# A two-layer hybrid decoder on one core: the keys' RMS norm as a factor along the free axis, applied where the logits leave PSUM

## The chip, the cores and the metric

One NeuronCore of a Trainium2 chip runs the whole computation as one program. The metric is the device time of one execution in microseconds. Of the kernel before, three runs took 2642.18, 2649.83 and 2652.11 us, median 2649.83 us.

## The reference

The input is one sequence of 1024 positions by 1024 channels, float32. Layer 0 is a gated DeltaNet with a SwiGLU FFN; layer 1 is stick-breaking attention over keys and values that are computed once, again with a SwiGLU FFN. The change touches the keys of layer 1:

```python
def rms_norm(x, gain):
    y = xf * lax.rsqrt(jnp.mean(xf * xf, axis=-1, keepdims=True) + EPS)
    return (y * gain.astype(jnp.float32)).astype(x.dtype)
...
    k, v = jnp.split(rms_norm(h, kv_norm) @ w_kv, 2, axis=-1)
    k = rms_norm(k.reshape(b_, s_, SB_HEADS, SB_DH), k_gain).transpose(0, 2, 1, 3)
...
        z = jnp.einsum('bhtd,bhsd->bhts', qb, kb) * scale
        ls_neg = jax.nn.log_sigmoid(-z)
        log_fail = jnp.where(causal, ls_neg, 0.0)
        log_rest = lax.cumsum(log_fail, axis=3, reverse=True) - log_fail
        log_a = z + ls_neg + log_rest
        att = jnp.where(causal, jnp.exp(log_a), 0.0)
```

There are 8 heads of 128 channels. A key's norm is one number for each head and each position s, so in the logits z[t, s] it is a factor that depends on the column s alone.

## The kernel before

The program runs in four stages: the DeltaNet mixer, its FFN, the attention ("sba") and the second FFN. Products that must be exact are made as three products of float32r parts, high by high, high by low and low by high, so a projection of one head (128 output channels, one half of 512 positions) is 8 times three products of 512 columns into a PSUM tile `ups` (`proj_half`, L135). Each engine executes its instructions in the order in which the program issues them.

In the attention stage (from L1458) the generators of one head's attention, `sb_steps(hd)`, and of the next head's projections, `qkv_steps(hd + 1)`, are interleaved by `merge` according to the costs that they yield. Work that hangs on a projection is put off by `post(delay, fn)` and taken up by `with_posts` once the projections' own clock has passed it.

- `k_take` (L1524) before the change: the head's keys, positions along the free axis and channels along the partitions, are copied to SBUF (L1550). `norm` transposes four blocks of 128 by 128 on PE (L1488), `row_norm` squares them on ACT (L1493), sums the rows on DVE (L1494) and takes (mean + EPS) to the power -0.5 on POOL with operands of 128x4 (L1495, L1496). `scale` multiplies the transposed keys by it on DVE (L1538). `back` transposes them back (L1488) and splits them with the gain into `kh` (L1545, ACT) and `kl` (L1546, DVE). That is done for each half of each head, 16 times.
- `sb_logs` (L1578): for block tb of 128 queries, the logits of up to 512 keys at a time in a PSUM tile `ips` (L1590 to L1592), out of which ACT takes the absolute value with the query's norm as scale into `l` (L1593) and DVE the scaled logits into `z` (L1594); then Exp and Ln over `l` (L1598, L1599).
- `sb_weights` (L1602): DVE adds max(z, 0) to `l` (L1607), POOL sets the part of the diagonal block that is not causal with two `affine_select` instructions of 128x128, first in `l`, then in `z` (L1609), DVE scans `l` backwards (L1613) and subtracts it from `z` (L1614), ACT takes Exp of `z` (L1616).
- `sb_transpose` (L1619) transposes `z` on PE (L1629) for the product with the values (`sb_values`, L1635). Block k's logits stand beside the weights of block k - 1, the transposes of block k - 2 and the values of block k - 3 (`sb_order`).
- `col_unit` (L115): a projection's raw weights are multiplied by the gain on POOL in four instructions of 128x256 (L121) before they are split.

POOL's power with a -0.5 operand is used in other places too: with 128x1 operands in the norms of rows (L208), with 128x4 in the DeltaNet mixer (L1176, L1321). PSUM has three tiles `ups` and five tiles `ips`.

Of the kernel before, what the change touches and what calls it, by code (L numbers as in the profile page):

```python
# [9 lines left out]
F32 = mybir.dt.float32  # L10
F32R = mybir.dt.float32r
U8 = mybir.dt.uint8
AF = mybir.ActivationFunctionType
ALU = mybir.AluOpType
# [4 lines left out]
P = 128  # L19
EPS = 1e-6  # L20
# [3 lines left out]
def yoco_kernel(  # L24
# [22 lines left out]
    act, dve, pool, pe, sp = nc.scalar, nc.vector, nc.gpsimd, nc.tensor, nc.sync  # L47
# [10 lines left out]
    HB = S // 2  # L58
# [16 lines left out]
    def i_tile(shape=(P, 4, P)):  # L75
        return pi.tile(list(shape), F32, tag="i", name="ips")

    def n_tile(shape=(P, S)):
        return main.tile(list(shape), F32, tag="n", name="n", bufs=4)
# [4 lines left out]
    def bc(ap, n=P):  # L84
        return ap.unsqueeze(2).broadcast_to([ap.shape[0], ap.shape[1], n])
# [4 lines left out]
    ones = cpool.tile([P, 1], F32, name="ones")  # L90
    pool.memset(ones, 1.0)
    mhalf = cpool.tile([P, 4], F32, name="mhalf")
# [78 lines left out]
    def run(gen):  # L171
        for _ in gen:
            pass
# [803 lines left out]
    with tc.tile_pool(name="gdn", bufs=1) as gp:  # L977
# [50 lines left out]
        def gain_cols(i, j, n):  # L1028
            return gains[:, offs[i] + j * n : offs[i] + (j + 1) * n]
# [4 lines left out]
        g_k = gain_cols(4, 0, 1)  # L1034

        norm = Norm(g_attn[0], False)
# [407 lines left out]
    with tc.tile_pool(name="ffn0", bufs=1) as hp:  # L1444
        norm, norm1 = PairNorm(g_ffn[0], hp), Norm(None)
# [12 lines left out]
    with tc.tile_pool(name="sba", bufs=1) as ap_:  # L1458
        tc.keep_in_program_order(act.preload_act_table_set("natural_log_exp_and_others"))

        def sb_tile(tag, nm):
            return ap_.tile([P, S], F32R, tag=tag, name=nm, bufs=4 if tag != "v" else 3)

        posts, clock = [], [0]
        POST, SCALE, BACK = 3000, 2000, 3000

        def post(delay, fn, *args):
            posts.append((clock[0] + delay, fn, args))
            posts.sort(key=lambda p: p[0])
# [15 lines left out]
        def transpose_half(f, hf):  # L1485
            tps = i_tile()
            for j in range(4):
                pe.transpose(tps[:, j, :], f[:, hf * HB + j * P : hf * HB + (j + 1) * P], ident)  # L1488
            return tps

        def row_norm(s_, tps):
            sq = main.tile([P, 4, P], F32, tag="og", name="sq")
            act.activation(sq, tps, AF.Square, scale=float(P) ** -0.5)  # L1493
            dve.tensor_reduce(s_, sq, axis=AX.X, op=ALU.add)  # L1494
            pool.tensor_scalar(s_, s_, EPS, None, op0=ALU.add)  # L1495
            pool.tensor_tensor(s_, s_, mhalf, op=ALU.pow)  # L1496

        def z_tile(tag):
            return ap_.tile([P, S], F32, tag=tag, name=tag, bufs=3 if tag == "z" else 2)

        def f_tile(hd):
            return z_tile("z") if hd == 0 else n_tile()

        def q_take(hd):
# [16 lines left out]
            qkv[hd, "q"] = (hi, lo, ss)  # L1521
            return take

        def k_take(hd):  # L1524
            f = f_tile(hd)
            hi, lo = sb_tile("k", "kh"), sb_tile("k", "kl")
            qkv[hd, "k"] = (hi, lo)

            def norm(hf):
                tps = transpose_half(f, hf)  # L1530
                ss = ap_.tile([P, 4], F32, tag="ss", name="ss", bufs=4)
                row_norm(ss, tps)
                post(SCALE, scale, hf, tps, ss)
                return 436

            def scale(hf, tps, ss):
                fs = f[:, hf * HB : (hf + 1) * HB].rearrange("p (a b) -> p a b", b=P)
                dve.tensor_tensor(fs, tps, bc(ss), op=ALU.mult)  # L1538
                post(BACK, back, hf)
                return 1  # L1540

            def back(hf):
                hs = slice(hf * HB, (hf + 1) * HB)
                tf = transpose_half(f, hf).rearrange("p a b -> p (a b)")
                act.activation(hi[:, hs], tf, AF.Copy, scale=g_k)  # L1545
                dve.scalar_tensor_tensor(lo[:, hs], tf, g_k, hi[:, hs], op0=ALU.mult, op1=ALU.subtract)  # L1546
                return 436

            def take(hf, sl, ps):
                act.copy(f[:, sl], ps)  # L1550
                post(POST, norm, hf)

            return take

# [18 lines left out]
        qkv, zs, ats, ofs = {}, {}, {}, {}  # L1573
# [3 lines left out]

        def sb_logs(hd, tb, later):  # L1578

            (qh, ql, qs), (kh, kl) = qkv[hd, "q"], qkv[hd, "k"]  # L1580
            w = (tb + 1) * P
            ts_ = slice(tb * P, (tb + 1) * P)
            z, l = z_tile("z"), z_tile("l")
            sc = qs[:, tb : tb + 1]
            next(later, None)
            for s0 in range(0, w, 512):
                n = min(512, w - s0)
                ss_ = slice(s0, s0 + n)
                zps = i_tile((P, 512))
                pe.matmul(zps[:, :n], qh[:, ts_], kh[:, ss_], start=True, stop=False)  # L1590
                pe.matmul(zps[:, :n], qh[:, ts_], kl[:, ss_], start=False, stop=False)
                pe.matmul(zps[:, :n], ql[:, ts_], kh[:, ss_], start=False, stop=True)  # L1592
                act.activation(l[:, ss_], zps[:, :n], AF.Abs, scale=sc)  # L1593
                dve.tensor_scalar(z[:, ss_], zps[:, :n], sc, None, op0=ALU.mult)  # L1594
                yield 3 * max(107, n * 0.417)
                next(later, None)
            run(later)
            act.activation(l[:, :w], l[:, :w], AF.Exp, scale=-1.0)  # L1598
            act.activation(l[:, :w], l[:, :w], AF.Ln, bias=1.0)  # L1599
            chains[hd, tb] = (z, l)  # L1600
# [53 lines left out]
        def sb_order():  # L1654

            blocks = [(hd, tb) for hd in range(H) for tb in range(NT)]
            n = len(blocks)
            for k in range(n + 3):
                at_ = blocks[min(k, n - 1)][0]
                later = sb_weights(*blocks[k - 1]) if 1 <= k < n + 1 else iter(())  # L1660
                yield at_, sb_logs(*blocks[k], later) if k < n else later
                if 2 <= k < n + 2:
                    yield at_, sb_transpose(*blocks[k - 2])
                if k >= 3 and blocks[k - 3][1] % 2:
                    hd, tb = blocks[k - 3]
                    yield at_, sb_values(hd, tb // 2)
# [14 lines left out]
        def head_all(hd):  # L1681
            takes = [k_take, q_take, v_take]
            if hd == 0:
                yield from proj_two_steps(norm1, [(la1.ready.pop(0), takes.pop(0)(hd)) for _ in range(2)])
                la1.fill(2)
            for take in takes:
                last = hd == H - 1 and take is takes[-1]
                for i, cost in enumerate(proj_steps(xT, la1.get(), take(hd))):
                    yield cost
                    if last and i in (1, KT + 1):  # L1690
                        next(fill)
# [39 lines left out]
    with tc.tile_pool(name="ffn1", bufs=1) as hp:  # L1731
        norm = PairNorm(g_ffn[1], hp)
# [34 lines left out]
```

## Time and profile before

| What | Value |
|---|---|
| runs of the kernel before, median | 2649.83 us |
| profiled execution, its own time | 2648.18 us |
| profiled execution, span | 2646.5 us |
| PE busy | 2539.9 us, 96% |
| DVE busy | 1844.0 us, 70% |
| ACT busy | 1144.9 us, 43% |
| POOL busy | 859.4 us, 32% |
| attention stage | about 1405 us to 1890 us |

The profile is of one execution, with times in microseconds from the span's start. PE is the engine of the matrix products, DVE the vector engine, ACT the scalar engine, POOL the general one, PEld the loading of weights into PE. Matmuls are pipelined, so the distance between two starts tells the cost of a product and not its listed duration. The profiled execution took 1.65 us less than the median.

### The profile page before, as it was taken

What the parts mean: (1) busy time and instruction counts of PE and PEld (TensorE: products, weight loads), DVE (VectorE), ACT (ScalarE), POOL (GpSimd) and SP (SyncE); (2) the same over time, 40 slices, a digit from 0 to 9 for tenths busy, and PEclk for the clock granted to TensorE, in tenths of its full rate; (3) what the DMA queues carried; (4) which work ended last, traced back from release to release, by engine and by line L of the source; (5) the groups of instructions that cost most, each with busy time, mean ns of one, the idle gap of its engine ahead of it and who ended that gap; (6) DMA issues with size and microseconds to landing.
All of it is one profiled execution on the core that took longest, in us unless ns stands there. A gap on an engine that the chain in (4) does not pass through costs nothing. (4 is left out here: it accounts for less than half of the span.)

```text
span 2646.5 us, 35828 instructions
## 1 busy us (share of the span) xinstructions
PE 2539.9 (96%) x12908; PEld 2067.5 (78%) x12908; DVE 1844.0 (70%) x2721; ACT 1144.9 (43%) x2219; POOL 859.4 (32%) x1262
## 2 busy tenths in 40 slices
PE   8999999999999999998999999999899999999999
PEld 6777878787768888886777778887776888887777
DVE  6667766775686666677755788877768566666774
ACT  6333333334363444432215666666536444443220
POOL 2444444444411222154313343342320222215420
PEclk9999999999999999999999999999999999999999
DMA  4211212223324554578661111112232455448766
GB/s 122 65 58 54 66 54 65 66 72 102 132 64 144 170 145 135 162 253 291 235 214 64 40 33 33 40 33 72 99 133 84 119 164 164 142 138 285 276 224 203
DMA packets 368952, 331.77 MB, mean 125 GB/s; under 512 B 19571, under 2 KB 321790, under 8 KB 368774
## 3 DMA queue, kind: packets, MB, share of 16 engines
q1 hardware_dynamic: 368774, 329.48, 39.5%
q8 instruction: 101, 1.65, 0.3%
q14 instruction: 77, 0.63, 0.1%
HBM read 226.37 MB, written 103.06 MB: 124 GB/s over the span
## 5 line engine op out<-in xcount | busy, mean ns | idle before, releaser
L140 PE MATMUL ups<-x,wh 128*128 128x512 f32 (+1 forms) x912 | 389.4, 428 | 0.0
L142 PE MATMUL ups<-x,wl 128*128 128x512 f32 (+1 forms) x912 | 363.6, 399 | 0.0
L141 PE MATMUL ups<-x,wh 128*128 128x512 f32 (+1 forms) x912 | 359.9, 395 | 0.0
L453 PE MATMUL ips<-x,w 128*128 128x512 f32 x840 | 328.7, 393 | 7.4 <-ACT x L359 3.7
L454 PE MATMUL ips<-x,w 128*128 128x512 f32 x840 | 329.1, 392 | 2.3 <-DVE x L360 2.3
L455 PE MATMUL ips<-x,w 128*128 128x512 f32 x840 | 328.3, 391 | 0.0
L552 POOL TENSOR_TENSOR n<-n,ev 128x512 f32<-128x512 f32 x44 | 70.7, 1606 | 626.5 <-ACT n L551 626.5
L453 PE MATMUL ups<-x,w 128*128 128x512 f32 x648 | 252.0, 392 | 1.7 <-ACT x L359 1.7
L454 PE MATMUL ups<-x,w 128*128 128x512 f32 x648 | 253.1, 391 | 0.0
L455 PE MATMUL ups<-x,w 128*128 128x512 f32 x648 | 252.3, 389 | 0.0
L142 PEld LDWEIGHTS ups<-x,wl 128*128 128x128 f32 (+1 forms) x912 | 171.1, 188 | 37.7
L453 PEld LDWEIGHTS ips<-x,w 128*128 128x128 f32 x840 | 157.8, 188 | 46.6 <-ACT x L359 6.2
L140 PEld LDWEIGHTS ups<-x,wh 128*128 128x128 f32 (+1 forms) x912 | 172.0, 189 | 22.7
L141 PEld LDWEIGHTS ups<-x,wh 128*128 128x128 f32 (+1 forms) x912 | 172.4, 189 | 21.3 <-DVE x L232 0.2
L454 PEld LDWEIGHTS ips<-x,w 128*128 128x128 f32 x840 | 158.3, 188 | 38.3 <-DVE x L360 4.9
L455 PEld LDWEIGHTS ips<-x,w 128*128 128x128 f32 x840 | 158.2, 188 | 32.9
L746 DVE TENSOR_TENSOR h<-h,ips 128x512 f32<-128x512 f32 x176 | 119.3, 682 | 61.0 <-PE ips L455 60.8
L453 PEld LDWEIGHTS ups<-x,w 128*128 128x128 f32 x648 | 121.5, 188 | 29.2 <-ACT x L359 4.0
L454 PEld LDWEIGHTS ups<-x,w 128*128 128x128 f32 x648 | 121.8, 188 | 26.8 <-DVE x L360 1.6
L455 PEld LDWEIGHTS ups<-x,w 128*128 128x128 f32 x648 | 121.7, 188 | 25.0
L746 DVE TENSOR_TENSOR h<-h,ups 128x512 f32<-128x512 f32 x136 | 92.6, 682 | 46.5 <-PE ups L455 46.3
L104 DVE TENSOR_TENSOR wl<-raw,wh 128x1024 fp32r<-128x1024 f32 x64 | 82.9, 1295 | 57.4 <-ACT wh L103 56.7
(364 smaller groups left out, 5991.7 us busy)
## 6 DMA issues: line engine op xcount, KB each, us to landing
raw<-in_ffn_w_gu_dram SPq DMA_DIRECT2D x88, 512.0 KB, 4.5
w<-hsa SPq DMA_DIRECT2D x88, 512.0 KB, 4.7
hsa<-w SPq DMA_DIRECT2D x116, 256.0 KB, 2.9
hb<-hsb SPq DMA_DIRECT2D x68, 384.0 KB, 4.0
raw<-in_ffn_w_down_dram SPq DMA_DIRECT2D x44, 512.0 KB, 4.3
raw<-in_gdn_w_in_dram SPq DMA_DIRECT2D x32, 512.0 KB, 4.1
hsb<-w SPq DMA_DIRECT2D x54, 256.0 KB, 3.6
hsa<-n SPq DMA_DIRECT2D x48, 256.0 KB, 3.6
```

What stands on the lines that cost most here:

```text
L104: dve.tensor_tensor(lo, raw, hi, op=ALU.subtract)
L140: pe.matmul(o, wh[:, kt, :m], xh, start=kt == 0, stop=False)
L141: pe.matmul(o, wh[:, kt, :m], xl, start=False, stop=False)
L142: pe.matmul(o, wl[:, kt, :m], xh, start=False, stop=kt == KT - 1)
L453: pe.matmul(ps, ah, bh, start=start, stop=False, skip_group_check=True)
L454: pe.matmul(ps, ah, bl, start=False, stop=False, skip_group_check=True)
L455: pe.matmul(ps, al, bh, start=False, stop=stop, skip_group_check=True)
L552: pool.tensor_tensor(s, s, self.t3, op=ALU.mult)
L746: dve.tensor_tensor(d, d, ps, op=ALU.add)
```

## The change

The keys are no longer normed before the logits. `kh` and `kl` are split straight from the projection's PSUM tile with the gain alone. Beside that ACT writes the squares, divided by 128, into a tile `sq`. `norm` sums them over the partitions by one float32 product with ones of 128x128 and 512 columns, so that every partition holds the sum of each position; ACT adds EPS on the way out of PSUM, and POOL takes the result to the power -0.5 in place, as a tile of 128x512 with the exponent broadcast. The tile `rk` so made (one tile for each head; a tile of tag `n`, for all heads but the first the same tile as `sq`) is a factor of the logits as they leave PSUM: one DVE instruction multiplies by the query's norm and by `rk`, and ACT takes the absolute value from `z` in SBUF afterwards.

```diff
-        POST, SCALE, BACK = 3000, 2000, 3000
+        POST = 3000
...
+        eps = ap_.tile([P, 1], F32, name="eps")
+        pool.memset(eps, EPS)
+
         def k_take(hd):
-            f = f_tile(hd)
+
             hi, lo = sb_tile("k", "kh"), sb_tile("k", "kl")
-            qkv[hd, "k"] = (hi, lo)
+            sq = f_tile(hd)
+            rk = [None if hd == 0 else sq]
+            qkv[hd, "k"] = (hi, lo, rk)
 
             def norm(hf):
-                tps = transpose_half(f, hf)
-                ss = ap_.tile([P, 4], F32, tag="ss", name="ss", bufs=4)
-                row_norm(ss, tps)
-                post(SCALE, scale, hf, tps, ss)
-                return 436
-
-            def scale(hf, tps, ss):
-                fs = f[:, hf * HB : (hf + 1) * HB].rearrange("p (a b) -> p a b", b=P)
-                dve.tensor_tensor(fs, tps, bc(ss), op=ALU.mult)
-                post(BACK, back, hf)
-                return 1
-
-            def back(hf):
                 hs = slice(hf * HB, (hf + 1) * HB)
-                tf = transpose_half(f, hf).rearrange("p a b -> p (a b)")
-                act.activation(hi[:, hs], tf, AF.Copy, scale=g_k)
-                dve.scalar_tensor_tensor(lo[:, hs], tf, g_k, hi[:, hs], op0=ALU.mult, op1=ALU.subtract)
-                return 436
+                if rk[0] is None:
+                    rk[0] = n_tile()
+                ms = i_tile((P, HB))
+                pe.matmul(ms, ones.broadcast_to([P, P]), sq[:, hs], start=True, stop=True)
+                act.activation(rk[0][:, hs], ms, AF.Identity, bias=eps)
+                pool.tensor_tensor(rk[0][:, hs], rk[0][:, hs], mhalf[:, 0:1].broadcast_to([P, HB]), op=ALU.pow)
+                return 908
 
             def take(hf, sl, ps):
-                act.copy(f[:, sl], ps)
-                post(POST, norm, hf)
+                act.activation(sq[:, sl], ps, AF.Square, scale=float(P) ** -0.5)
+                act.activation(hi[:, sl], ps, AF.Copy, scale=g_k)
+                dve.scalar_tensor_tensor(lo[:, sl], ps, g_k, hi[:, sl], op0=ALU.mult, op1=ALU.subtract)
+                post(POST if hd else 2 * POST, norm, hf)
 
             return take
...
-            (qh, ql, qs), (kh, kl) = qkv[hd, "q"], qkv[hd, "k"]
+            (qh, ql, qs), (kh, kl, (rk,)) = qkv[hd, "q"], qkv[hd, "k"]
...
-                act.activation(l[:, ss_], zps[:, :n], AF.Abs, scale=sc)
-                dve.tensor_scalar(z[:, ss_], zps[:, :n], sc, None, op0=ALU.mult)
+                dve.scalar_tensor_tensor(z[:, ss_], zps[:, :n], sc, rk[:, ss_], op0=ALU.mult, op1=ALU.mult)
+                act.activation(l[:, ss_], z[:, ss_], AF.Abs)
```

The other costs that `norm` returns move the steps of `merge` against each other. The rows below are of the attention of head 2 and the projections of head 3, a pair of streams that stands for those of the heads after it. A tile's number tells one buffer's use from another; the numbers differ between the kernels.

POOL, before the change, from the third block of head 2 (`l_14487`, `z_14486`) to the sixth (`l_14684`); `ss` is the norm of the keys of head 3, `raw` a raw weight:

```order
L1609 AFFINE_SELECT l_14487<-l_14487 128x128
L1609 AFFINE_SELECT z_14486<-z_14486 128x128
L1495 TENSOR_SCALAR ss_14534<-ss_14534 128x4
L1496 TENSOR_TENSOR ss_14534<-ss_14534,mhalf_76 128x4
L1609 AFFINE_SELECT l_14571<-l_14571 128x128
L1609 AFFINE_SELECT z_14570<-z_14570 128x128
L121 TENSOR_TENSOR raw_15174<-raw_15174,gains_123 128x256 x4
L1609 AFFINE_SELECT l_14616<-l_14616 128x128
L1609 AFFINE_SELECT z_14615<-z_14615 128x128
L1495 TENSOR_SCALAR ss_14658<-ss_14658 128x4
L1496 TENSOR_TENSOR ss_14658<-ss_14658,mhalf_76 128x4
L1609 AFFINE_SELECT l_14684<-l_14684 128x128
```

POOL, after the change, the same place: `l_14414` is the third block of head 2, `l_14487` now the fourth, `l_14534` the fifth, and `n_14301` is the tile `rk` of head 3:

```order
L1606 AFFINE_SELECT l_14414<-l_14414 128x128
L1606 AFFINE_SELECT z_14413<-z_14413 128x128
L1541 TENSOR_TENSOR n_14301<-n_14301,mhalf_76 128x512
L1606 AFFINE_SELECT l_14487<-l_14487 128x128
L1606 AFFINE_SELECT z_14486<-z_14486 128x128
L121 TENSOR_TENSOR raw_15069<-raw_15069,gains_123 128x256 x4
L1541 TENSOR_TENSOR n_14301<-n_14301,mhalf_76 128x512
L1606 AFFINE_SELECT l_14534<-l_14534 128x128
L1606 AFFINE_SELECT z_14533<-z_14533 128x128
```

The power of four columns has become one of 512, in front of the selects of the fourth and of the fifth block; between the two powers stand the selects of one block and the four instructions of one raw weight.

DVE, after the change, from the fourth block's `l` to the place behind the fifth block's subtraction (L1610 is the scan, L1611 the subtraction, L1590 the eviction of logits, `attl` the low part of transposed weights):

```order
L1604 SCALAR_TENSOR_TENSOR l_14487<-z_14486,l_14487 128x512
L1590 SCALAR_TENSOR_TENSOR z_14533<-ips_14554,ssq_13953,n_13737 128x128
L1610 SCALAR_TENSOR_TENSOR l_14487<-l_14487 128x512
L1629 TENSOR_TENSOR attl_14564<-ips_14565,atth_14563 128x3x128
L1611 TENSOR_TENSOR z_14486<-z_14486,l_14487 128x512
L1604 SCALAR_TENSOR_TENSOR l_14534<-z_14533,l_14534 128x640
L1590 SCALAR_TENSOR_TENSOR z_14587<-ips_14594,ssq_13953,n_13737 128x512
L1610 SCALAR_TENSOR_TENSOR l_14534<-l_14534 128x640
L1611 TENSOR_TENSOR z_14533<-z_14533,l_14534 128x640
L1590 SCALAR_TENSOR_TENSOR z_14587<-ips_14608,ssq_13953,n_13737 128x256
```

Each scan reads what POOL's select has written, and the evictions of PSUM tiles behind it on DVE follow it in order, as they did before. On PE, from the first product with ones of head 3 to the transposes of the fourth block (`z_14486`) stand 39 products of 512 columns, 18 of 256, 9 of 128, five transposes and the second product with ones; to the transposes of the fifth block (`z_14533`) four transposes, 15 products of 512 and 3 of 384 columns more.

PE, after the change, the end of the stretch to the fourth block's transposes:

```order
L1643 MATMUL ips_14575<-atth_14434,vh_14200 128x256
L1644 MATMUL ips_14575<-attl_14435,vh_14200 128x256
L1645 MATMUL ips_14575<-atth_14434,vl_14201 128x256
L1539 MATMUL ips_14579<-n_14301,ones_74 128x512
...
L1587 MATMUL ips_14608<-kh_13735,qh_13951 128x256
L1588 MATMUL ips_14608<-kl_13736,qh_13951 128x256
L1589 MATMUL ips_14608<-kh_13735,ql_13952 128x256
L1626 MATMUL ips_14617<-ident_69,z_14486 128x128 x4
```

The second product with ones stands ahead of the transposes that need the selects behind the first power.

## Rows read from the trace of the kernel before

**Rows 1.** The page, busy time of two engines (share of span, instructions):

```profile
PE 2539.9 (96%) x12908; PEld 2067.5 (78%) x12908; DVE 1844.0 (70%) x2721; ACT 1144.9 (43%) x2219; POOL 859.4 (32%) x1262
```

**Rows 2.** Stretches: us, busy us (instructions) by engine, PE clock; one head, an early stretch.

```profile
core 0: us, PE busy (x) PEld busy (x) DVE busy (x) ACT busy (x) POOL busy (x), PEclk, DMA share, GB/s
1502.45:1560.12 57.67, 54.93 (x309) 46.67 (x309) 45.79 (x63) 38.71 (x71) 20.28 (x33) 1.00 0.12 37
...
50.00:60.00 10.00, 8.39 (x43) 6.81 (x42) 8.51 (x13) 5.12 (x16) 0.10 (x1) 0.83 0.38 109
```

**Rows 3.** Waits, 1405 to 1890 us: who waited for whom: us, times, longest.

```profile
POOL l L1609 <- DVE l L1607: 176.1, 44, 9.4
...
DVE l L1613 <- POOL l L1609: 21.9, 29, 2.4
...
PE ips L1590 <- DVE kl L1546: 6.3, 6, 1.2
...
PE ips L1488 <- DVE n L1538: 1.6, 1, 1.6
```

**Rows 4.** Single lines, POOL's powers and a multiply: ns minimum, median, maximum; starts.

```profile
L208 POOL TENSOR_TENSOR nss<-nss,mhalf x32: 549/569/1018, 5.6 to 1986.7; 128x1 f32<-128x1 f32 x32
...
L1496 POOL TENSOR_TENSOR ss<-ss,mhalf x16: 1037/1038/1044, 1410.4 to 1812.5; 128x4 f32<-128x4 f32 x16
...
L1177 POOL TENSOR_SCALAR rk<-rk x16: 223/230/252, 62.5 to 608.5; 128x4 f32<-128x4 f32 x16
```

**Rows 5.** Groups by form, POOL: out<-in, shape, count | busy us, mean ns | idle before.

```profile
L552 POOL TENSOR_TENSOR n<-n,ev 128x512 f32<-128x512 f32 x44 | 70.7, 1606 | 626.5 <-ACT n L551 626.5
...
L1217 POOL TENSOR_TENSOR um<-tc,mdiag 128x512 f32<-128x512 f32 x16 | 20.7, 1295 | 1.3
...
L1215 POOL TENSOR_TENSOR tc<-tc,pr 128x60 f32<-128x60 f32 x16 | 5.0, 315 | 1.3
...
L1215 POOL TENSOR_TENSOR tc<-tc,pr 128x4 f32<-128x4 f32 x16 | 3.4, 212 | 1.2
```

**Rows 6.** Groups by form, POOL: raw weights by the gain, and the select.

```profile
L121 POOL TENSOR_TENSOR raw<-raw,gains 128x256 f32<-128x256 f32 x96 | 77.2, 833 | 74.5 <-DMA raw<-in_w_kv_dram 58.9 <-DMA raw<-in_sb_w_q_dram 8.6 <-ACT n L1650 4.0
...
L1609 POOL TENSOR_SCALAR_AFFINE_SELECT l<-l 128x128 f32<-128x128 f32 x64 | 19.1, 299 | 176.1 <-DVE l L1607 176.1
```

**Rows 7.** Groups by form, 1270 to 1960 us: DVE's scan and subtraction, ACT.

```profile
L1613 DVE TENSOR_TENSOR_SCAN l<-l 128x640 f32<-128x640 f32 x8 | 12.3, 1536 | 6.6 <-POOL l L1609 6.6
...
L1614 DVE TENSOR_TENSOR z<-z,l 128x640 f32<-128x640 f32 x8 | 6.5, 812 | 0.0
...
L1493 ACT ACTIVATE sq<-ips 128x512 f32<-128x512 f32 x32 | 19.2, 600 | 14.0 <-PE ips L1488 14.0
...
L1616 ACT ACTIVATE z<-z 128x640 f32<-128x640 f32 x8 | 5.9, 740 | 14.7 <-DVE z L1614 14.7
```

**Rows 8.** Timeline of PE in head 1's attention: start us, duration us, line, out<-in.

```profile
1504.48 0.60 PE L1629 MATMUL ips<-ident,z 128*128 128x128 f32 x4
1504.83 0.48 PE L140 MATMUL ups<-x,wh 128*128 128x512 f32 x1
1505.15 0.39 PE L141 MATMUL ups<-x,wh 128*128 128x512 f32 x1
1505.38 0.39 PE L142 MATMUL ups<-x,wl 128*128 128x512 f32 x1
1505.61 0.34 PE L1590 MATMUL ips<-kh,qh 128*128 128x384 f32 x1
1505.79 0.35 PE L1591 MATMUL ips<-kl,qh 128*128 128x384 f32 x1
...
1508.01 0.28 PE L1646 MATMUL ips<-atth,vh 128*128 128x256 f32 x1
1508.13 0.28 PE L1647 MATMUL ips<-attl,vh 128*128 128x256 f32 x1
```

**Rows 9.** Timeline of PE in the first stage: four float32 products of 128 columns.

```profile
328.36 1.05 PE L1143 MATMUL ips<-y 128*128 128x128 f32 x8
329.17 0.47 PE L140 MATMUL ups<-x,wh 128*128 128x512 f32 x1
```

## The prediction

> **What bounds the kernel now.** I read the page's busy times first: PE is busy in 96% of the span, POOL in 32% [rows 1]. By stretches, one head of the attention takes 57.67 us, in which PE is busy 54.93, DVE 45.79, ACT 38.71 and POOL 20.28 us [rows 2]. So PE sets the pace, and a gain has to come out of PE's work or PE's waits. The view of waits tells what little waiting there is. PE lost 6.3 us to `kl` and 1.6 us to the scaled keys in the whole stage; DVE's scan waited 21.9 us for POOL's select; and POOL waited 176.1 us for the input of that select [rows 3]. The reader is to see in this that POOL has much idle time, but that it stands inside the chain of every block: DVE's `l`, POOL's selects, DVE's scan and subtraction, ACT's Exp, PE's transposes. Idle time of such an engine is room for many short instructions and for no long one, since it works in order.
>
> **The change part by part.** The largest question is the new power on POOL, 128x512, 16 times. The nearest rows are powers of the same kind on narrower tiles: 569 ns for one column and 1038 ns for four, with minimum and median a few ns apart for the wide one [rows 4]. Three columns more cost 469 ns, 156.3 ns each. That is not what POOL takes for other things: a multiply or add of four columns takes 212 to 230 ns [rows 4, 5], one of 60 columns 315 and one of 512 columns 1295 [rows 5], (1295 - 212) / 508 = 2.1 ns a column. So the power has a price by the column, some 73 times that of a multiply, and nothing in the narrow rows says that it ends at four. Drawn on: 569 + 511 x 156.3 ns = 80.5 us for each. The bounds lie far apart. Below, a power costs a multiply's 1.6 us [rows 5]; above, four columns are the unit of work and all of it repeats, 1038 / 4 = 259.5 ns a column, 133 us. I take 80.5, because it is the line through the two rows of the same operation.
>
> [...]
>
> What of a power lies on the path: the selects behind it wait, the scan waits for them on DVE with evictions behind it, and PE comes to the transposes of that block and stops. I follow one pair of powers, from the end of the first product with ones, for the heads 2 to 7. ACT takes the sums out of PSUM in 0.6 us (as the squares [rows 7]); the power 80.5; two selects 0.6 and the raw weight's four instructions 3.3 [rows 6]; the second power, whose input has long been ready, 80.5; then a select 0.3 [rows 6], the scan of 640 columns 1.54, the subtraction 0.81, Exp 0.74 [rows 7], together 3.4. That is 168.9 us, after which PE may transpose the fifth block. PE has other work up to there: 54 products of 512 columns at 0.23 us from start to start, 3 of 384 at 0.18, 18 of 256 at 0.12, four transposes in 0.35 us, so 9 of them in 0.8 [rows 8], 9 of 128 columns, which I put at 0.1 between 256 columns and nothing, and the second product with ones, 0.81 by four float32 products of 128 columns [rows 9]: 12.4 + 0.5 + 2.2 + 0.8 + 0.9 + 0.8 = 17.6 us. The pair adds 168.9 - 17.6 = 151.3 us; six of them 907.8. The evictions that PE needs within these 17.6 us stand ahead of the waiting scans on DVE, or the five PSUM tiles suffice for them.
>
> The pair of head 1 has more on PE up to the first transposes behind its second power (137 products of 512 columns, 3 of 384, 27 of 256, 9 of 128, 34 transposes, one product with ones: 40.1 us by the same prices). The pair of head 0 runs before any attention and its first transposes come after 113 of 512, 3 each of 384, 256 and 128, 16 transposes and one product with ones: 29.4 us. Their POOL rows differ by some microseconds (wider blocks, a weight more), so I use 168.9 for both: 128.8 and 139.5. All eight: 907.8 + 128.8 + 139.5 = **1176 us**.
>
> The smaller terms. On PE a half of the keys loses eight transposes, twice 0.35 us [rows 8], and gains the product with ones, 0.81 [rows 9]: 0.1 us more, 16 times, 1.6 us. The waits for the scaled keys and for `kl` [rows 3] can go: 7.9 us less at most, which I take. [...] Eight returns after the second powers: 0 to 14 us, and I take 14. [...] DVE loses a reduction and a multiply for each half, ACT exchanges a copy for the evicted sums: both stay below PE's 54.93 us a head [rows 2], so I cost them at nothing; without PE's cover DVE would be next, at 45.79. The absolute value now follows the logits' eviction and does not run beside it, which lengthens a block's chain by less than the 0.6 us of an ACT pass [rows 7], two blocks ahead of its transposes: nothing. `rk` keeps a tile of tag `n` for a whole head; if a later tile had to wait for it, that would be a loss, which I leave to the upper end. No DMA is added or moved; raw weights behind a power come late, but their split is due after the stop that the power causes anyway.
>
> Sum: 1176 + 1.6 - 7.9 + 14 = 1184 us. The profiled execution took 2648.2 us, 1.65 below the median of the runs: 2648.2 + 1184 = **3832 us**. A tenth more or less in the price of a column moves this by 16 x 8 = 128 us, and if PE's work covers nothing, it rises by 6 x 17.6 + 40.1 + 29.4 = 175 us. So this case reaches by itself from 3700 to 4007 us.
>
> **The rivals.** First, a power of 512 columns is as cheap as a multiply, 1.6 us. Then POOL keeps its idle time, the selects wait 1.6 us at most where they waited before for a power of 1.04, and the product with ones and the ended waits remain: 2648.2 + 1.6 - 7.9 = 2642 us, not slower. It decides from the point at which a power is short against the 13 us of PE work ahead of the first transposes (39 products of 512 columns, 18 of 256, 9 of 128, five transposes, one with ones). For it speaks that all other two-input work of POOL is cheap and that much of 569 ns may be a start; against it, the difference of 469 ns for three columns, in which no start is left.
>
> Second, long rows are cheaper by the column than short ones, say by half (an unrolled loop that four columns don't fill): 0.6 + 511 x 0.078 = 40.5 us, 40 us less for each of 16, and 3832 - 640 = 3192 us. With other fractions anything from 2700 to 3700. For it speaks only that four columns are few; against it, that multiplies keep the same price from 4 and 60 to 512 columns.
>
> Third, the cover is gone: DVE stands at the scan, the PSUM tiles behind it fill, and PE stops at once. That is the 175 us above: 4007 us. Against it speaks that four PSUM tiles of five are taken when PE gets to the transposes.
>
> **How the numbers follow.** My forecast has 0.75, the cheap power 0.08, the half price 0.12, the lost cover 0.05. About 0.5% of the time, 13 us, is what a measurement of this kernel can tell from no change. The cheap power's 2642 us lies within that; with some waits more gone it may pass below 2635, so of its 0.08 I put 0.06 on the same and 0.02 on faster. All else is slower: 0.92. The range goes from 3300 to 4010: nearly all of the forecast's case (0.73), a third of the half price (0.04), more than half of the lost cover (0.03), 0.80 together. The forecast's own range is 3700 to 4007.
>
> **What would show it.** The new power as a group of 16 on POOL with a mean near 80 us; POOL busy near 2100 us; PE busy still near 2540 us, but two thirds of the span; in the waits DVE's scan for POOL's select as the largest, near 1100 us, with ACT's Exp and PE's transposes behind it; eight pairs of stops in the attention stage, each near 150 us, at a lowered PE clock after them. Wrong would be: a mean of a few us, a mean that is not near 156 ns times 512, or PE idle time much below or above what the powers last.

## The result, and the profile after

The changed kernel takes 3880.03 us (median of five runs, 3877.75 to 3880.81) against 2649.83 us, the median of five as well: 1.4652 times the time before, 95% interval 1.4633 to 1.4671. The forecast was 3832 us in a range from 3300 to 4010. The profiled execution took 3877.85 us, 1229.7 more than that of the kernel before.

The page's busy times and its costliest groups answer to [rows 1] and [rows 4]; in the groups the columns are line, engine, operation, shapes and count, then busy us and mean ns of one, then the idle time before them and what ended it:

```profile
PE 2573.1 (66%) x12812; PEld 2084.4 (54%) x12812; DVE 1835.9 (47%) x2689; ACT 1139.2 (29%) x2219; POOL 2153.4 (56%) x1247
...
L1541 POOL TENSOR_TENSOR n<-n,mhalf 128x512 f32<-128x512 f32 x16 | 1317.2, 82328 | 13.6 <-ACT n L1540 13.6
L1626 PE MATMUL ips<-ident,z 128*128 128x128 f32 x288 | 55.3, 311 | 1069.7 <-ACT z L1613 1069.7
L1610 DVE TENSOR_TENSOR_SCAN l<-l 128x128 f32<-128x128 f32 (+3 forms) x64 | 89.2, 1394 | 1198.1 <-POOL l L1606 1197.8
```

Sixteen powers take 82.3 us each, 1317 us in all, and POOL's busy time grew by 1294 us from 859.4: the powers are the whole of it. PE has about the work it had and is now busy in 66% of the span. The idle time moved to the chain behind POOL: DVE's scan waits 1197.8 us for POOL's select, where it waited 21.9 before [rows 3], and PE's transposes wait 1069.7 us for ACT's Exp, which comes after the scan.

One pair of powers in POOL's timeline (start us, duration us, line, out<-in, and in brackets the idle time before), of the attention of head 3 with the powers of head 4:

```profile
2236.16 0.29 POOL L1606 TENSOR_SCALAR_AFFINE_SELECT z<-z 128x128 f32<-128x128 f32 x1
2236.42 82.57 POOL L1541 TENSOR_TENSOR n<-n,mhalf 128x512 f32<-128x512 f32 x1
2318.96 0.29 POOL L1606 TENSOR_SCALAR_AFFINE_SELECT l<-l 128x128 f32<-128x128 f32 x1
2319.20 0.29 POOL L1606 TENSOR_SCALAR_AFFINE_SELECT z<-z 128x128 f32<-128x128 f32 x1
2319.46 4.35 POOL L121 TENSOR_TENSOR raw<-raw,gains 128x256 f32<-128x256 f32 x4
2323.77 81.91 POOL L1541 TENSOR_TENSOR n<-n,mhalf 128x512 f32<-128x512 f32 x1
2405.65 0.29 POOL L1606 TENSOR_SCALAR_AFFINE_SELECT l<-l 128x128 f32<-128x128 f32 x1
...
2450.64 82.57 POOL L1541 TENSOR_TENSOR n<-n,mhalf 128x512 f32<-128x512 f32 x1
```

PE's timeline in the same pair:

```profile
2234.14 1.02 PE L1539 MATMUL ips<-n,ones 128*128 128x512 f32 x2
2234.59 0.68 PE L1643 MATMUL ips<-atth,vh 128*128 128x256 f32 x1
2235.11 0.28 PE L1644 MATMUL ips<-attl,vh 128*128 128x256 f32 x1
...
2248.36 0.28 PE L1589 MATMUL ips<-kh,ql 128*128 128x256 f32 x1
2322.33 1.12 PE L1626 MATMUL ips<-ident,z 128*128 128x128 f32 x4 [73.69 <-ACT z L1613]
2323.10 0.78 PE L140 MATMUL ups<-x,wh 128*128 128x512 f32 x1
...
2328.10 0.40 PE L142 MATMUL ups<-x,wl 128*128 128x512 f32 x1
2409.28 1.11 PE L1626 MATMUL ips<-ident,z 128*128 128x128 f32 x4 [80.78 <-ACT z L1613]
```

The reader is to see two stops, 73.69 and 80.78 us, each in front of the transposes of a block whose select stood behind a power. Between the product with ones and the first stop PE has its 13.6 us of other work, between the two stops 6. From one head's first power (2236.42) to the next (2450.64) pass 214.2 us; before, a head took 57.67 [rows 2].

The stretches of that head (us; busy us and instructions of each engine; PE's granted clock; DMA share; GB/s):

```profile
2235.00:2321.00 86.00, 13.64 (x74) 11.26 (x72) 10.22 (x15) 8.87 (x17) 85.08 (x7) 0.59 0.04 12
2321.00:2329.00 8.00, 6.16 (x22) 4.92 (x22) 2.43 (x4) 2.00 (x4) 8.00 (x4) 0.71 0.00 0
2329.00:2409.00 80.00, 0.00 (x0) 0.00 (x0) 2.92 (x4) 0.51 (x1) 77.19 (x3) 0.52 0.00 0
2409.00:2420.00 11.00, 10.72 (x50) 9.22 (x50) 9.00 (x13) 8.93 (x17) 2.95 (x6) 0.75 0.00 1
2420.00:2449.30 29.30, 28.46 (x155) 23.49 (x154) 20.03 (x27) 17.72 (x35) 10.79 (x17) 1.00 0.13 37
```

While PE stands in the third stretch, its granted clock is 0.52 of full; behind the second stop it is 0.75 over eleven microseconds, 0.50 from 2409.28 to 2414.40 among them, and then 1.00. In the third stretch POOL alone is at work, 77.19 of 80 us; DVE has 2.92, ACT 0.51 and PE nothing.

The powers of head 1, beside head 0's attention, stop PE at other places. Of the waits in the stage (who waited for whom: us, times, longest), two single ones are theirs, and DVE's timeline shows what held the first:

```profile
PE ips L1488 <- ACT n L1565: 80.2, 10, 73.7
...
PE ips L1539 <- DVE attl L1629: 75.4, 1, 75.4
...
1685.06 1.82 DVE L1610 TENSOR_TENSOR_SCAN l<-l 128x768 f32<-128x768 f32 x1 [78.45 <-POOL l L1606]
1686.81 0.66 DVE L1629 TENSOR_TENSOR attl<-ips,atth 128x512 fp32r<-128x512 f32 x1
```

Here PE stops already at the second product with ones (L1539), because DVE stands at the scan and the copy `attl`, which frees a PSUM tile, stands behind that scan. So the second power's input is late, and the two powers of this head lie 7.4 us apart, where those of head 4 lie 4.8. The second stop, 73.7 us, is at the transposes of the values, which wait for ACT's copy behind Exp.

### The profile page after: what moved, and what is told of

It reads as the page before. It is cut to its first block, busy times and chain, and to the rows that moved or that the text cites. A ratio compares the mean times of both kernels' runs of the same rounds, so it can differ in the third digit from the quotient of the medians.

```text
span 3876.1 us, 35606 instructions
## 1 busy us (share of the span) xinstructions
PE 2573.1 (66%) x12812; PEld 2084.4 (54%) x12812; DVE 1835.9 (47%) x2689; ACT 1139.2 (29%) x2219; POOL 2153.4 (56%) x1247
## 5 line engine op out<-in xcount | busy, mean ns | idle before, releaser
L1541 POOL TENSOR_TENSOR n<-n,mhalf 128x512 f32<-128x512 f32 x16 | 1317.2, 82328 | 13.6 <-ACT n L1540 13.6
L1626 PE MATMUL ips<-ident,z 128*128 128x128 f32 x288 | 55.3, 311 | 1069.7 <-ACT z L1613 1069.7
L1610 DVE TENSOR_TENSOR_SCAN l<-l 128x128 f32<-128x128 f32 (+3 forms) x64 | 89.2, 1394 | 1198.1 <-POOL l L1606 1197.8
L1626 PEld LDWEIGHTS ips<-ident,z 128*128 128x128 f32 x288 | 39.6, 158 | 1084.7 <-ACT z L1613 1077.6
L1613 ACT ACTIVATE z<-z 128x128 f32<-128x128 f32 (+3 forms) x64 | 43.7, 683 | 1253.2 <-DVE z L1611 1253.2
L140 PE MATMUL ups<-x,wh 128*128 128x512 f32 (+1 forms) x912 | 397.0, 436 | 0.0
L141 PE MATMUL ups<-x,wh 128*128 128x512 f32 (+1 forms) x912 | 366.0, 402 | 0.0
L140 PEld LDWEIGHTS ups<-x,wh 128*128 128x128 f32 (+1 forms) x912 | 176.7, 194 | 25.1 <-issue 0.5
L141 PEld LDWEIGHTS ups<-x,wh 128*128 128x128 f32 (+1 forms) x912 | 176.7, 194 | 23.9 <-issue 0.5
```

The source lines that it names most:

```text
L140: pe.matmul(o, wh[:, kt, :m], xh, start=kt == 0, stop=False)
L141: pe.matmul(o, wh[:, kt, :m], xl, start=False, stop=False)
L1541: pool.tensor_tensor(rk[0][:, hs], rk[0][:, hs], mhalf[:, 0:1].broadcast_to([P, HB]), op=ALU.pow)
L1610: dve.tensor_tensor_scan(rv, rv, rv, 0.0, op0=ALU.add, op1=ALU.bypass)
L1613: act.activation(z[:, :w], z[:, :w], AF.Exp)
L1626: pe.transpose(tps[:, j, :], z[:, (j0 + j) * P : (j0 + j + 1) * P], ident)
```

## The experiments

The theory was that POOL's power has a price by the column, and that everything behind it on an engine that works in order waits for it. The rivals: that a part of the loss lies in the rest of the change; that the price is one of the instruction or of the stop and not of the columns.

### The power as a multiply

```diff
-                pool.tensor_tensor(rk[0][:, hs], rk[0][:, hs], mhalf[:, 0:1].broadcast_to([P, HB]), op=ALU.pow)
+                pool.tensor_tensor(rk[0][:, hs], rk[0][:, hs], mhalf[:, 0:1].broadcast_to([P, HB]), op=ALU.mult)
```

> The changed kernel with one word changed: POOL multiplies the 512 columns by the broadcast operand where it took them to a power, so the keys' norm is left out and all else of the change stays. Theory of the prediction (the price of a power by the column, in front of selects on an engine that works in order, is the whole loss): the new instruction takes 1.3 to 1.6 us and the time falls from 3880 to 2642 us, between 2630 and 2655. Rival (a good part of the 1230 us comes from the rest of the change: the product with ones, the eviction on DVE with the absolute value behind it, the tile kept for a head): above 2680 us, with PE waits in the attention stage that the kernel before did not have.

Measured: 2657.76 us against 2648.78, ratio 1.0034 (1.0022 to 1.0047). One word, with which the kernel leaves out the keys' norm, takes 1222 of the 1230 us away. The group of 16 on POOL is now

```profile
L1541 POOL TENSOR_TENSOR n<-n,mhalf 128x512 f32<-128x512 f32 x16 | 22.7, 1418 | 15.6 <-ACT n L1540 15.6
```

1.4 us in place of 82.3. But the time lies 3 us over the range that was expected: what is left of the change, POOL's multiply of 512 columns included, is not the gain of 6 us that was reckoned but costs 9 us.

### The power on half of the columns

```diff
-                pool.tensor_tensor(rk[0][:, hs], rk[0][:, hs], mhalf[:, 0:1].broadcast_to([P, HB]), op=ALU.pow)
+                h0 = slice(hf * HB, hf * HB + HB // 2)
+                pool.tensor_tensor(rk[0][:, h0], rk[0][:, h0], mhalf[:, 0:1].broadcast_to([P, HB // 2]), op=ALU.pow)
```

> The changed kernel with the power on the first 256 of each half's 512 columns only; the other 256 keep mean plus EPS, so half of the keys are not normed. Price by the column at 160 ns: 41.3 us for each of 16, 41 us less each, 16 x 41 = 656 us less: 3224 us. Rival one (the instruction has a large fixed part): over 3500 us. Rival two (fewer columns are hidden better, since PE's own work covers a fixed 17 us of a pair): that cover is already full, so no difference from the first.

Measured: 3229.29 us in one run, where 3224 was expected. Half of the columns took about half of the loss away. The group:

```profile
L1542 POOL TENSOR_TENSOR n<-n,mhalf 128x256 f32<-128x256 f32 x16 | 664.5, 41532 | 13.7 <-ACT n L1540 13.7
```

Each power is 82.3 - 41.5 = 40.8 us shorter; 16 of them make 653 us, and the time fell by 651. A microsecond of power was a microsecond of the kernel, so the cover by PE's own work is indeed used up already and the same for both.

### The price at eight widths

```diff
+        probe = half("um").rearrange("p a b -> p (a b)")
+        pool.memset(probe, 3.7)
+        pool.tensor_tensor(probe[:, 0:1], probe[:, 0:1], mhalf[:, 0:1].broadcast_to([P, 1]), op=ALU.pow)
...
+        pool.tensor_tensor(probe[:, 0:256], probe[:, 0:256], mhalf[:, 0:1].broadcast_to([P, 256]), op=ALU.mult)
```

> The kernel before, with powers of 1, 2, 4, 8, 16, 64, 256 and 512 columns of a tile of 3.7 and multiplies of 4, 16 and 256 columns added on POOL at the start, none of them used. A straight line through 569 ns for one and 1038 ns for four columns gives 0.57, 0.73, 1.04, 1.66, 2.9, 10.4, 40.4 and 80.5 us. Rival (short rows pay a start that long ones don't, or long rows cost more by the column): the wide ones lie off the line; 41.6 us at 256 and 82.3 at 512, read already from two kernels, would put the step between 4 and 256 columns. Multiplies: 0.2, 0.3 and 0.8 us.

The groups by shape, POOL, of that kernel (the last two are multiplies):

```profile
L993 POOL TENSOR_TENSOR um<-um,mhalf 128x1 f32<-128x1 f32 x1 | 0.6, 552 | 0.0
...
L994 POOL TENSOR_TENSOR um<-um,mhalf 128x2 f32<-128x2 f32 x1 | 0.9, 853 | 0.0
...
L995 POOL TENSOR_TENSOR um<-um,mhalf 128x4 f32<-128x4 f32 x1 | 1.0, 1018 | 0.1
...
L996 POOL TENSOR_TENSOR um<-um,mhalf 128x8 f32<-128x8 f32 x1 | 1.6, 1634 | 0.1
...
L997 POOL TENSOR_TENSOR um<-um,mhalf 128x16 f32<-128x16 f32 x1 | 2.9, 2894 | 0.1
...
L998 POOL TENSOR_TENSOR um<-um,mhalf 128x64 f32<-128x64 f32 x1 | 10.5, 10518 | 0.1
...
L999 POOL TENSOR_TENSOR um<-um,mhalf 128x256 f32<-128x256 f32 x1 | 41.1, 41125 | 0.1
...
L1000 POOL TENSOR_TENSOR um<-um,mhalf 128x512 f32<-128x512 f32 x1 | 81.9, 81915 | 0.1
...
L1001 POOL TENSOR_TENSOR um<-um,mhalf 128x4 f32<-128x4 f32 x1 | 0.2, 201 | 0.1
...
L1003 POOL TENSOR_TENSOR um<-um,mhalf 128x256 f32<-128x256 f32 x1 | 1.0, 995 | 0.1
```

It is a straight line but for the row of two columns, which lies 0.15 us over it: (1018 - 552) / 3 = 155 ns a column at the narrow end, (81915 - 41125) / 256 = 159 at the wide end. No width is clearly cheaper by the column than the line says. A multiply of 256 columns takes 1.0 us, a power 41.1. The whole kernel took 2787.89 us in one run, 140 us over the runs beside it. That is the sum of these powers, which stand between the first norms' short powers on POOL.

### Four pieces for each power, spread over the blocks

```diff
-                pool.tensor_tensor(rk[0][:, hs], rk[0][:, hs], mhalf[:, 0:1].broadcast_to([P, HB]), op=ALU.pow)
+                for j in range(4):
+                    post(2500 * j + 5000 * hf, piece, hf * HB + j * P)
                 return 908

+            def piece(c):
+                cs = slice(c, c + P)
+                with ExitStack() as es:
+                    if sel[0] is not None:
+                        es.enter_context(tc.issue_after(sel[0].ins))
+                    pool.tensor_tensor(rk[0][:, cs], rk[0][:, cs], mhalf[:, 0:1].broadcast_to([P, P]), op=ALU.pow)
+                return 1
```

> The changed kernel with each power of 512 columns made as four of 128 that are spread over the blocks of the head before: on POOL there stand two, one, two and three of them between the selects of successive blocks. The same columns are taken to the power, so POOL works as long. Theory (a stop costs what POOL takes less the PE work that runs under it): four stops a head in place of two have some 7 us of PE work each under them, so a head falls from 214 by some 15 us, and the time by some 100 to 130: 3750 to 3790 us. Rival (what counts is that PE stops at all, with a price for each stop in clock and drained queues): not faster than 3880, and up to 3950 us.

Measured: 3799.9 us, ratio 1.4345 (1.4318 to 1.4373), 80 us less than the changed kernel. POOL's timeline of one head:

```profile
2012.61 42.06 POOL L1551 TENSOR_TENSOR n<-n,mhalf 128x128 f32<-128x128 f32 x2
...
2059.95 21.88 POOL L1551 TENSOR_TENSOR n<-n,mhalf 128x128 f32<-128x128 f32 x1
...
2082.30 42.83 POOL L1551 TENSOR_TENSOR n<-n,mhalf 128x128 f32<-128x128 f32 x2
...
2127.04 63.81 POOL L1551 TENSOR_TENSOR n<-n,mhalf 128x128 f32<-128x128 f32 x3
...
2213.72 21.36 POOL L1551 TENSOR_TENSOR n<-n,mhalf 128x128 f32<-128x128 f32 x1
```

A head takes 2213.72 - 2012.61 = 201.1 us in place of 214.2, 13 less (15 expected). PE has four stops a head here in place of two. More stops with PE work under each are better than fewer, so the rival of a price for each stop falls. The whole gain is 80 us and not 100 to 130: six heads at 13 us make it, and the first two give nothing (their stops last 147 and 152 us, before 145 and 149). The expectation also took POOL to work as long as before, but 64 pieces of 21.2 us hold it for 1358 us, 41 more than the sixteen powers.

### Ln and Exp on ACT

```diff
-                act.activation(rk[0][:, hs], ms, AF.Identity, bias=eps)
-                pool.tensor_tensor(rk[0][:, hs], rk[0][:, hs], mhalf[:, 0:1].broadcast_to([P, HB]), op=ALU.pow)
+                act.activation(rk[0][:, hs], ms, AF.Ln, bias=eps)
+                act.activation(rk[0][:, hs], rk[0][:, hs], AF.Exp, scale=-0.5)
```

> The changed kernel with the power taken off POOL: ACT takes Ln of the sums plus EPS on the way out of PSUM and then Exp with scale -0.5, so the norm is computed in full by another engine. If POOL's power is the whole loss: one ACT pass of 0.6 us more for each of 16 halves, on an engine that is busy 38.7 of 57.7 us a head, so nothing on the path: 2642 us, between 2630 and 2655, as the multiply. Rival (the two functions bring table loads, 1.28 us each as the one of the attention stage in the trace, up to 32 of them, in front of evictions that PE waits for): 2660 to 2685 us.

Measured: 2652.63 us against 2648.78, ratio 1.0008 (0.9999 to 1.0017), with the norm in full. The attention stage has the one table load it had (L1459, 1283 ns at 1404.1 us). So the same change with the power on another engine costs nothing that these runs can tell from the kernel before, and gains nothing either. With the multiply the ratio to the same runs was 1.0034 (1.0022 to 1.0047), which this one's interval does not touch, so a part of those 9 us went with POOL's instruction of 512 columns; through which wait is not shown. Of its waits, who waited for whom, two are PE's:

```profile
PE ips L1488 <- ACT n L1565: 15.4, 9, 2.7
PE ips L1626 <- ACT z L1613: 11.6, 13, 2.4
```

PE waits 15.4 us for the values' copy out of PSUM, which the kernel before did not show.

### Where the small loss lies: the eviction alone, and the values later

In the first of two kernels the kernel before has the new order of the eviction alone:

```diff
-                act.activation(l[:, ss_], zps[:, :n], AF.Abs, scale=sc)
                 dve.tensor_scalar(z[:, ss_], zps[:, :n], sc, None, op0=ALU.mult)
+                act.activation(l[:, ss_], z[:, ss_], AF.Abs)
```

> The kernel before with one part of the change alone: DVE evicts the scaled logits first and ACT takes the absolute value from them in SBUF, in place of both reading PSUM; the keys' norm stays where it was. If the lengthened chain is what ate the waits that the cheap versions should have saved (they came out 4 to 9 us over the kernel before, not 6 under): 2655 to 2665 us, with ACT waiting for DVE's logits 30 us and more in the attention stage. If it costs nothing, as the prediction had it: 2645 to 2653 us.

Measured: 2647.39 us against 2647.51, ratio 0.9997 (0.9987 to 1.0007). ACT does wait for DVE's logits (40.8 us in the stage), and it costs nothing: that theory of mine fell. In the second, the version with Ln and Exp has the values' transposes later:

```diff
-                post(POST, rows, hf)
+                post(POST + 2000, rows, hf)
```

> The version with Ln and Exp on ACT, with the transposes of the values put off by 5000 in place of 3000 of the projections' clock. In that version PE waited 15 us for ACT's copies of the values out of PSUM, which the kernel before did not. If these waits come from the place of the transposes alone, they go and the time falls from 2652.6 by 10 to 15 us: 2638 to 2643 us, under the kernel before. If ACT is late for another reason that moves with the stage, PE waits elsewhere: 2648 to 2656 us.

Measured: 2647.76 us, ratio 1.0002 (0.9992 to 1.0012). The waits for the copies fell from 15.4 to 1.8 us; PE then waited 5.0 us for `attl` and, as without this edit, 11.1 for Exp. By the medians the time fell by 5 us, half of what was expected, but the two ratios, 0.9999 to 1.0017 and 0.9992 to 1.0012, overlap: a gain from this edit is not shown.

### The sum over the partitions in one pass

```diff
-            sq = f_tile(hd)
-            rk = [None if hd == 0 else sq]
+            sq = (ap_.tile([P, S], F32R, tag="z", name="sqz", bufs=3) if hd == 0
+                  else main.tile([P, S], F32R, tag="n", name="sqn", bufs=4))
+            rk = [None]
...
-                pe.matmul(ms, ones.broadcast_to([P, P]), sq[:, hs], start=True, stop=True)
+                pe.matmul(ms, ones_r.broadcast_to([P, P]), sq[:, hs], start=True, stop=True)
```

> The version with Ln and Exp on ACT and the later transposes of the values, with the squares written as float32r and summed by one float32r product of 512 columns in place of the float32 one; the squares are rounded to float32r by that, and the norm has a tile of its own. The float32 product holds PE for 0.81 us, a float32r one of 512 columns for 0.23 us. If PE's work is what sets the time again, as in the kernel before: 16 x 0.58 = 9 us less than 2647.8: 2638 to 2640 us, the first version clearly under the kernel before. Rival (the fifth tile of tag n for each head makes a later copy out of PSUM wait, and PE with it): 2645 us and more, with PE waiting for ACT's copies.

Measured: 2628.57 us against 2648.03, ratio 0.9933 (0.9919 to 0.9946). That is under both kernels, by 19 us under the one before, with the squares written as float32r. PE's timeline shows the product, 0.23 us from start to start:

```profile
1505.56 0.39 PE L1542 MATMUL ips<-sqn,ones_r 128*128 128x512 f32 x1
1505.79 0.27 PE L1646 MATMUL ips<-atth,vh 128*128 128x256 f32 x1
```

Its expectation reckoned 9 of these 19 us. A last kernel has the second tile alone, with the float32 product:

```diff
-            rk = [None if hd == 0 else sq]
+            rk = [None]
```

> The version with the later transposes of the values and with squares and norm in two tiles of tag n, as in the version with the float32r sum, but with the float32 product. That version came out 19 us under this one's parent, where the shorter product explains 9. If the second tile gives the rest (by another order of the steps, or since the squares' tile comes free early): 2637 to 2640 us. If the whole 19 us hang on the product (PE's order shifts with it): 2646 to 2650 us, as the parent.

Measured: 2645.84 us against 2647.32, ratio 0.9992 (0.9983 to 1.0001). The tile is worth 2 us by the medians, which is not clear of noise; 16 or 17 hang on the product, of which 0.58 us for each of 16 explain 9. What the other 7 or 8 are stays open; no run here shows it.

## Why the prediction was right, and where it was off

- **The bound and the chain.** PE sets the pace and POOL stands inside the chain of every block: shown by the multiply, which gives back 1222 us, and by the waits after, in which scan, Exp and transposes stand idle one behind the other.
- **The price of the power.** The step that decided, the straight line through the rows for one and four columns, held over 128 times the width: 80.5 us said, 82.3 measured. The rivals of a cheap power and of a cheaper wide one fell to the rows of eight widths. The first rival took the power to cost what a multiply costs: at 512 columns the multiply took 1.4 us and the power 82.3.
- **The cover, heads 2 to 7.** From the product with ones to the transposes of the fifth block 168.9 us were reckoned. The product ended near 2235.0 (0.81 us after its start), the transposes began at 2409.28: 174.3 us. Of the difference of 5.4, the two powers make 3.5, the raw weight's instructions 1.1 (4.35 us for 3.3), the start of the first power, for which POOL had two selects to end, 0.8. PE's work under the first power was 13.6 us, 13.3 said. In these heads PE ran on to the first transposes that needed a select.
- **The cover, head 1.** Here the step that evictions stand ahead of the waiting scan or the PSUM tiles suffice was wrong, and the third rival came true in part for this one head: PE ran on for 10.6 us behind the first product with ones and stopped at the second, behind DVE's `attl`. The step that the second power's input has long been ready fell with it.
- **Head by head.** PE's instructions are the same, in the same order, in the changed kernel and in the kernel with the multiply, so their starts can be set side by side. The changed kernel is 3.4 us early before head 0's stop, 140.1 us late before head 1's, 295.0 late before head 2's, and 1219.6 late at the end. So head 0's pair costs 143.5 us (139.5 said), head 1's 154.9 (128.8 said) and the other six 924.6 (907.8 said), 47 us more in all.
- **The clock.** No run shows the 14 us that stand in the sum for eight returns of PE's clock, 1.75 us each. The clock did fall, as was expected: in the head above 0.75 was granted over the 11 us behind the second stop, 0.50 up to 2414.40 and 1.00 from 2414.50 on, which by estimate from that 0.75 are 2.8 us at most for one return. But such losses did not stay in the time. Set beside the kernel with the multiply, in the heads 2 to 7 PE loses 1.6 to 2.7 us there and has most or all of them back before the next head's first stop: at the transposes of the values (L1488) that kernel waits 2.3 to 2.8 us for ACT's copy, and the changed kernel 0.1 to 1.3.
- **What was off.** The sum was 1184, measured 1229.7. The pairs cost 47 us more than said: 16 x 1.8 = 29 are the power's price, and most of the rest, some 21, is head 1's early stop. The clock's 14 are missing. The small terms make 15: I took 6.3 us of gain (1.6 of product less 7.9 of ended waits), and the kernel with the multiply shows 9 of loss. 47 - 14 + 15, less the 3.4 us that this execution was ahead, are 45 of the 46. That the forecast came so near is in part luck, since the clock's 14 us, which did not come, stood in for a part of the rest. The waits for the scaled keys went, but others came in their place, for the values' copies (15.1 us with the multiply) and for Exp (16.5): I took the end of old waits as a gain and looked for no new one there. The eviction alone cost nothing, and with the norm on ACT no loss is shown; which wait makes the 9 us stays open.

## What to carry to other kernels

Price an operation from rows of that operation, and ask two widths of it for the slope: here POOL takes 201 ns for a multiply of 4 columns and 995 for one of 256, 3 ns a column, and 160 ns a column for a power. A long instruction on an engine that works in order was paid here by whoever waited for the short ones behind it (DVE's scan stood 1197.8 us), less the work that the waiting engine had left (PE's 20 us of 174 in a pair), however idle the engine looked in the page. A power for each position was cheap on POOL where it was narrow (128x4, 1.0 us) and dear once it was spread over 128x512 (82.3 us); as Ln and Exp on ACT the wide one cost nothing that could be measured.

## What the runs showed of the hardware

- POOL's power takes 552 ns for one column of 128 partitions; between the rows of 4, 8, 16, 64, 256 and 512 columns each column more takes 154 to 160 ns. Its multiply at 256 columns takes 1.0 us.
- PE's granted clock was 0.52 in a stretch of 80 us in which PE had nothing to do, then 0.75 in the eleven microseconds behind the stop, 0.50 in the first 5.1 of them, and 1.00 in the stretch after.
- Of the six kernels near the time before, the one with the float32r sum gained 7 or 8 us more than the shorter product explains. I had not expected that and have no row for it.
